# A longer planned distance between attention scores and the transposes of their softmax, and a third buffer for rows of p, in a one-core hybrid encoder layer

## The chip, the cores and the metric

The kernel runs on one core of a Trainium2 chip. The metric is the device time of one execution in microseconds (us). Five engines work side by side: TensorE (PE, with its weight loads shown as PEld), VectorE (DVE), ScalarE (ACT), GpSimd (POOL) and SyncE (SP), which issues DMAs. Each engine has a queue of its own, worked off in order; semaphores tie the queues together.

## The reference

One layer of a streaming encoder, for a prompt of 512 rows and a sample batch of 32 rows, which share all weights (544 columns in the kernel's transposed layout). All data are float32; D_MODEL is 1024, there are 16 heads of 64 in each mixer, the ConvFFN is 2816 wide.

```
h = rmsnorm(x)
z = h @ w_in                      # q_a k_a v_a q_b k_b v_b gate_a gate_b
# mixer A: 16 q heads on 4 kv heads, own chunk of 64 + 2 chunks before, ALiBi, a sink in the softmax
# mixer B: 16 heads, own chunk + 8 chunks before, learned relative bias
q, k = rmsnorm per head of q, k
p = softmax(q @ k.T * 64**-0.5 + bias)
o = p @ v
x = x + (sigmoid(gate_a) * o_a + sigmoid(gate_b) * o_b) @ w_out
[a | b] = causal depthwise conv3(rmsnorm(x) @ w_up)
x = x + (gelu(a) * b) @ w_down
```

The sample rows attend to given caches of k and v too. New rows of k, v and of the convolution are outputs as well.

## The kernel before

**Dense products.** The projection by `w_in` is cut into 52 tiles of 128 output rows, `w_out` into 8, `w_up` into 44, and so on. `dense` (L232) computes one tile in two halves of 272 columns, each in one PSUM bank. Float32 accuracy comes from a split of both operands into a high and a low part in the type fp32r: `triple` (L220) issues hi x hi, hi x lo and lo x hi, so that a half is 8 x 3 = 24 products and a tile 48. The moving operands are called xh and xl (s in `w_out` and behind), the weights w_hi and w_lo. `prep` (L192) makes them from a loaded w_raw: POOL rounds w_hi (L201), VectorE subtracts w_lo (L204); each has two buffers, so that a weight can be made only once the last product with the weight two tiles earlier is done. All matmuls are recorded in one helper line, L85, all transposes in L89.

**What is between the dense products.** A tile of q or k goes through `head_norm` (L401): ScalarE reads the bank twice (a square, L411, and z, L412), POOL splits the square (t_sqh L413, t_sql L414), PE takes two products with a block matrix of ones into a bank st, `newton` (L312) makes the reciprocal root of it (t_y and t_b; VectorE's part, L319, reads the bank again), POOL multiplies z by t_y (L421), VectorE writes zn (L422), and `write` splits it into the stacks q (L445, L446) or k (L429 to L431), of which one half is copied to the other partitions by a DMA (`dup`, L434).

An attention head of the prompt is `attend_prompt` (L528): four score tiles into four banks, from which VectorE writes p with the bias added and the row maximum taken (L501); the softmax in place on p (exponentials on ScalarE L485, the scaling by the reciprocal sum on POOL L493); transposes of p on PE into two or three banks, each evacuated as pt_h and pt_l (L511, L512); the output products with v into one more bank, and `fold` (L515; t_o L519, s L520). There are 16 such heads in mixer A and 16 in mixer B. `attend_sample` (L560) does the same for the sample rows of several heads at once, with p_s in place of p.

**What sets the order.** The class `Stream` (L69) keeps a clock of its own, in microseconds, that each recorded matmul moves on. An attention head is a generator; where it says `yield LAT_SOFT`, it is put aside until the clock has gone on by that amount. After each triple of a dense tile, `pe.step()` takes up one task that is due, or starts the next head of a queue. So the LAT constants say how many dense products are written between two steps of a head. The softmax itself is issued at a low priority (`LATER`). Behind that, the framework's scheduler takes the recorded program, its priorities, buffers and its own estimate of times, and decides the final order on every engine; the recorded order is thus its input and not its result.

**Banks and buffers.** Dense halves use a pool of 3 PSUM banks (`psd`); everything else, the norms, scores, transposes and outputs, shares 5 (`psa`). Tiles of the attention come from the pool `ap`, with two buffers each unless a number is given. `p` is a tile of 128 x 1280 float32 values, 5 KB in each partition.

**The end of the stretch.** The last products of `w_in` and the last heads end near 485 us. Then the `w_out` tiles begin: the first two are interleaved over three banks (L871 to L883) with the products of the gates (`s`, L827) cut into high and low parts as they come ready, and the results are added to x by VectorE (L898).

Of the kernel before, what the change touches and what calls it, by code (L numbers as in the profile page):

```python
# [8 lines left out]
F32 = mybir.dt.float32  # L9
# [44 lines left out]

LAT_FIRST, LAT_ROW = 9.15, 0.35
LAT_SQ, LAT_NORM, LAT_DMA = 2.9, 6.89, 3.63
LAT_Z, LAT_SOFT, LAT_PT = 6.55, 9.34, 4.75
LAT_SOFT_S, LAT_PTS = 8.46, 1.1
PACE_A, PACE_B, PACE_S = 7.09, 5.87, 1.44

WARM = 7
# [82 lines left out]
def body(ctx, tc, a, o):  # L144
# [16 lines left out]
    def bank(pool):  # L161
        return pool.tile([128, 512], F32, name="ps")
# [204 lines left out]
    ap = att.enter_context(tc.tile_pool(name="ap", bufs=2))  # L367
# [110 lines left out]
    def softmax(p, tiles, mx, sinkcol):  # L478

        n = len(tiles)  # L480
        nm = ap.tile([128, 4], F32, name="nm", bufs=3)[:, :n]
        V.tensor_scalar(nm, mx, -1.0, 1.0, ALU.mult, ALU.mult)  # L482
        sm = ap.tile([128, 4], F32, name="sm", bufs=4)[:, :n]
        for t, sl in enumerate(tiles):
            act(p[:, sl], p[:, sl], AF.Exp, bias=nm[:, t:t + 1], accum_out=sm[:, t:t + 1])  # L485
        if sinkcol is not None:
            es = ap.tile([128, 4], F32, name="es", bufs=3)[:, :n]
            act(es, nm, AF.Exp, bias=sinkcol)
            V.tensor_tensor(sm, sm, es, ALU.add)
        rc = ap.tile([128, 4], F32, name="rc", bufs=3)[:, :n]  # L490
        V.reciprocal(rc, sm)  # L491
        for t, sl in enumerate(tiles):
            G.tensor_scalar(p[:, sl], p[:, sl], rc[:, t:t + 1], 1.0, ALU.mult, ALU.mult)  # L493

    def scores(out, lhs, rhs, bias, floor, mx):
        ps = bank(psa)
        n = len(lhs)
        for i in range(n):
            mm(ps[:, :rhs[i].shape[1]], lhsT=lhs[i], rhs=rhs[i], start=i == 0, stop=i == n - 1)
        ps = ps[:, :out.shape[1]]  # L500
        V.tensor_tensor_reduce(out=out, in0=ps, in1=bias, op0=ALU.add, op1=ALU.max, scale=1.0,  # L501
                               scalar=floor, accum_out=mx)

    def transposed(p, blocks, n):

        ps = bank(psa)
        for src, dst in blocks:
            transpose(ps[:, dst:dst + 128], p[:, src:src + 128], ident)
        h = ap.tile([128, 512], F32R, name="pt_h", bufs=3)
        l = ap.tile([128, 512], F32R, name="pt_l", bufs=3)  # L510
        nc.scalar.copy(h[:, :n], ps[:, :n])  # L511
        V.tensor_tensor(l[:, :n], ps[:, :n], rr(h)[:, :n], ALU.subtract)  # L512
        return h, l

    def fold(po, dst, hh, n):  # L515

        own, other = ((slice(0, 64), slice(64, 128)), (slice(64, 128), slice(0, 64)))[hh]
        t = ap.tile([128, 512], F32, name="t_o", bufs=2)
        nc.scalar.copy(t[own, :n], po[other])  # L519
        V.tensor_tensor(dst[own], po[own], t[own, :n], ALU.add)  # L520
# [7 lines left out]
    def attend_prompt(q, kh, kl, bias, floor, sinkcol, geo, groups, vt, hh, dst, dh, scored, done):  # L528


        p = ap.tile([128, 1280], F32, name="p")
        mx = ap.tile([128, 4], F32, name="mx", bufs=4)
        tiles = []
        for t, (pc, k0, n, bc) in enumerate(geo):
            qs = q[:, 128 * t:128 * t + 128]
            scores(p[:, pc:pc + n], [qs, qs], [x[:, k0:k0 + max(n, 256)] for x in (kh, kl)], bias[:, bc:bc + n],
                   floor, mx[:, t:t + 1])
            tiles.append(slice(pc, pc + n))
        scored()
        with tc.high_priority(LATER):  # L540
            softmax(p, tiles, mx, sinkcol)
        yield LAT_SOFT
        pts = []
        for blocks, n, _ in groups:
            pts.append(transposed(p, blocks, n))
        yield LAT_PT
        po = bank(psa)
        started = False
        last = groups[-1][2][-1]
        for (h, l), (_, _, prods) in zip(pts, groups):  # L550
            for pr in prods:
                j, c, oc, w = pr
                for x in (h, l):
                    mm(po[:, oc:oc + w], lhsT=vt[:, j, hh, :, :], rhs=x[:, c:c + w],
                       start=not started, stop=pr is last and x is l, skip_group_check=True)
                    started = True
        fold(po, dst[:, :NP], dh, NP)
        done()
# [132 lines left out]
    def group_a(j, ka, va):  # L691
# [25 lines left out]
        for u in range(2):  # L717
            pe.reserve("q", 2, 5)
            st2 = [ap.tile([128, NP], F32R, name="q", bufs=5) for _ in range(2)]
            ready = []  # L720
            qready.append(ready)

            def sample(zn, u=u):
                for hh, own, other in pair_rows():
                    h = 2 * u + hh
                    nc.scalar.copy(qsam[own, h], zn[own])
                    V.tensor_tensor(qsam[other, h], zn[own], rr(qsam)[own, h], ALU.subtract)
            for hh in range(2):
                h = 4 * j + 2 * u + hh

                def start(bias, u=u, hh=hh, st2=st2, h=h):
                    sc = col("sink", h)
                    return attend_prompt(st2[hh], kh, kl, bias, sc, sc, a_geo, a_groups, vt, half,
                                         oa[u], hh, scored, finished)
                pe.queue(lambda h=h: fetch("bias", h, 512, a["alibi"][h]), start, (ready, ka[2], va[2]), PACE_A)
            dense(head_norm(0, load_q(st2, sample, ready)))
# [28 lines left out]
    def pair_b(i, ob, one):  # L765
# [48 lines left out]
        for hh in range(2):  # L814
            def start(bias, hh=hh):
                return attend_prompt(st2[hh], kh[hh], kl[hh], bias, -3.0e38, None, b_geo, b_groups, vt, hh,
                                     ob, hh, scored, finished)
            pe.queue(lambda hh=hh: fetch("bias", i, 512, a["rel"][2 * i + hh]), start, (qr, kr, vr), PACE_B)
# [413 lines left out]
```

## Time and profile before

| what | us |
|---|---|
| median of 3 runs (lowest, highest) | 924.7 (921.4, 926.1) |
| profiled execution, its time | 924.88 |
| profiled execution, its span in the trace | 923.0 |
| PE busy (multiplications) | 898.6 |
| PEld busy | 884.4 |
| DVE busy | 723.6 |
| ACT busy | 542.2 |
| POOL busy | 379.1 |

The mean granted clock of TensorE over the span was 0.994 of full speed. A busy engine is one that executes an instruction; the span is the time between the first and the last record of the execution. In the rows further down, a number in square brackets at a row's end is the time that the engine stood idle just before the instruction, followed by the instruction that released it.

### The profile page before, as it was taken

What the parts mean: (1) busy time and instruction counts of PE and PEld (TensorE: products, weight loads), DVE (VectorE), ACT (ScalarE), POOL (GpSimd) and SP (SyncE); (2) the same over time, 40 slices, a digit from 0 to 9 for tenths busy, and PEclk for the clock granted to TensorE, in tenths of its full rate; (3) what the DMA queues carried; (4) which work ended last, traced back from release to release, by engine and by line L of the source; (5) the groups of instructions that cost most, each with busy time, mean ns of one, the idle gap of its engine ahead of it and who ended that gap; (6) DMA issues with size and microseconds to landing.
All of it is one profiled execution on the core that took longest, in us unless ns stands there. A gap on an engine that the chain in (4) does not pass through costs nothing.

```text
span 923.0 us, 18908 instructions
## 1 busy us (share of the span) xinstructions
PE 898.6 (97%) x7085; PEld 884.4 (96%) x7085; DVE 723.6 (78%) x1471; ACT 542.2 (59%) x1285; POOL 379.1 (41%) x578
## 2 busy tenths in 40 slices
PE   8879999999999999999999999999999999999998
PEld 7879899989989999999999999999999999999998
DVE  7799876868888888998866558768777776886996
ACT  5568777778878777777764244344444443534542
POOL 6534457465876777766541103221222221100100
PEclk9999999999999999999999999999999999999999
DMA  6222222322334443434415222222222222332342
GB/s 216 83 82 88 71 90 85 101 81 75 109 118 122 135 124 109 129 110 136 133 59 168 89 92 92 92 77 85 92 93 92 84 87 83 96 101 81 119 145 67
DMA packets 40012, 94.38 MB, mean 102 GB/s; under 512 B 4944, under 2 KB 16240, under 8 KB 39920
## 3 DMA queue, kind: packets, MB, share of 16 engines
q1 hardware_dynamic: 39920, 93.17, 31.8%
q8 instruction: 56, 0.92, 0.4%
q14 instruction: 36, 0.29, 0.1%
HBM read 80.48 MB, written 7.10 MB: 95 GB/s over the span
## 4 chain that ended last, share of the span: by engine, by line
PE 76%; DVE 9%; ACT 4%; POOL 3%; issue 2%; DMA 0%; DVEq 0%; POOLq 0%
PE ps L85 73%; PE ps L89 3%; ACT p L485 2%; DVE q L446 1%; DVE zn L422 1%; DVE p L501 1%; DVE w_lo L204 1%; POOL p L493 1%; DVE s L254 1%; DVE t_b L319 1%; DVE k L431 1%; POOL t_sql L414 1%; POOL z L421 1%; DVE pt_l L512 0%; DMA k<-k 0%
## 5 line engine op out<-in xcount | busy, mean ns | idle before, releaser
L85 PE MATMUL ps<-xh,w_lo 128*128 128x272 f32 x1536 | 446.3, 292 | 5.1 <-DVE w_lo L204 5.1
L85 PE MATMUL ps<-xh,w_hi 128*128 128x272 f32 x1536 | 446.0, 292 | 2.7 <-ACT z L412 1.7
L85 PE MATMUL ps<-xl,w_hi 128*128 128x272 f32 x1536 | 446.3, 291 | 0.8 <-DVE xl L327 0.8
L85 PEld LDWEIGHTS ps<-xh,w_lo 128*128 128x128 f32 x1536 | 291.6, 190 | 6.5 <-DVE w_lo L204 6.0
L85 PEld LDWEIGHTS ps<-xh,w_hi 128*128 128x128 f32 x1536 | 291.5, 190 | 4.8 <-ACT z L412 1.9
L85 PEld LDWEIGHTS ps<-xl,w_hi 128*128 128x128 f32 x1536 | 292.0, 190 | 2.1 <-DVE xl L327 1.7
L204 DVE TENSOR_TENSOR w_lo<-w_raw,w_hi 128x1024 fp32r<-128x1024 f32 (+2 forms) x112 | 143.2, 1279 | 30.8 <-ACT w_hi L203 18.3
L201 POOL TENSOR_SCALAR w_hi<-w_raw 128x1024 fp32r<-128x1024 f32 (+2 forms) x62 | 66.6, 1075 | 90.2 <-PE ps L85 70.3
L493 POOL TENSOR_SCALAR p<-p,rc 128x256 f32<-128x256 f32 (+3 forms) x128 | 74.2, 596 | 41.4 <-DVE rc L491 38.0
L203 ACT CAST w_hi<-w_raw 128x1024 fp32r<-128x1024 f32 x50 | 52.6, 1051 | 64.9 <-issue 36.1
L85 PE MATMUL ps<-s,w_hi 128*128 128x272 f32 x448 | 84.0, 288 | 0.0
L485 ACT ACTIVATE p<-p,nm 128x256 f32<-128x256 f32 (+3 forms) x128 | 65.4, 514 | 27.8 <-DVE nm L482 27.7
L938 POOL TENSOR_SCALAR state_u<-u 128x2 f32<-128x2 f32 x44 | 17.1, 388 | 148.7 <-DVE u L935 148.7
L85 PE MATMUL ps<-s 128*128 128x272 f32 (+1 forms) x483 | 71.3, 293 | 1.7 <-DVE s L372 1.7
L85 PEld LDWEIGHTS ps<-s,w_hi 128*128 128x128 f32 x448 | 70.1, 188 | 0.0
L935 DVE TENSOR_TENSOR u<-ps,rstd 128x272 f32<-128x272 f32 x88 | 38.5, 441 | 39.6 <-PE ps L85 37.0
L85 PEld LDWEIGHTS ps<-s 128*128 128x128 f32 x483 | 65.1, 190 | 2.2 <-DVE s L372 1.7
L85 PE MATMUL ps<-s,w_lo 128*128 128x272 f32 x224 | 63.8, 288 | 0.0
L85 PE MATMUL ps<-k,q 128*128 128x256 f32 (+2 forms) x256 | 52.1, 308 | 3.5 <-DMA k<-k 1.8
L414 POOL TENSOR_TENSOR t_sql<-t_sq,t_sqh 128x272 fp32r<-128x272 f32 x52 | 52.7, 1014 | 3.7
L421 POOL TENSOR_TENSOR z<-z,t_y 128x272 f32<-128x272 f32 x52 | 42.7, 822 | 23.9 <-ACT t_y L316 21.7
L512 DVE TENSOR_TENSOR pt_l<-ps,pt_h 128x512 fp32r<-128x512 f32 (+1 forms) x80 | 45.6, 602 | 5.5 <-ACT pt_h L511 4.4
(166 smaller groups left out, 1635.1 us busy)
## 6 DMA issues: line engine op xcount, KB each, us to landing
w_raw<-in_w_in SPq DMA_DIRECT2D x50, 512.0 KB, 3.4
w_raw<-in_w_up SPq DMA_DIRECT2D x44, 512.0 KB, 3.3
w_raw<-in_w_pair SPq DMA_DIRECT2D x16, 512.0 KB, 3.4
k<-k SPq DMA_DIRECT2D x40, 128.0 KB, 2.3
bias<-in_rel SPq DMA_DIRECT2D x16, 256.0 KB, 2.7
w_raw<-in_w_out SPq DMA_DIRECT2D x8, 512.0 KB, 3.5
s<-in_x SPq DMA_DIRECT2D x15, 272.0 KB, 5.7
w_raw<-in_w_down SPq DMA_DIRECT2D x6, 512.0 KB, 3.3
```

The costliest lines, as they stand in the source:

```text
L85: return self.nc.tensor.matmul(out, lhsT=lhsT, rhs=rhs, **kw)
L89: return self.nc.tensor.transpose(out, src, ident)
L201: G.tensor_scalar(hi[:, c], raw[:, c], 1.0, 1.0, ALU.mult, ALU.mult)
L203: nc.scalar.copy(hi[:, c], raw[:, c])
L204: V.tensor_tensor(lo[:, c], raw[:, c], rr(hi)[:, c], ALU.subtract)
L414: G.tensor_tensor(sql, sq, rr(sqh), ALU.subtract)
L421: G.tensor_tensor(z, z, y, ALU.mult)
L485: act(p[:, sl], p[:, sl], AF.Exp, bias=nm[:, t:t + 1], accum_out=sm[:, t:t + 1])
L493: G.tensor_scalar(p[:, sl], p[:, sl], rc[:, t:t + 1], 1.0, ALU.mult, ALU.mult)
L512: V.tensor_tensor(l[:, :n], ps[:, :n], rr(h)[:, :n], ALU.subtract)
L935: V.tensor_tensor(u[:, 2 + c0:2 + c0 + cn], ps, rstd2[:, c0:c0 + cn], ALU.mult)
L938: G.tensor_scalar(state_u[:, m, 0:2], u[:, NP:NP + 2], 1.0, 1.0, ALU.mult, ALU.mult)
```

## The change

Three numbers are changed. `LAT_SOFT`, the planned time from the last score of a prompt head to the first transpose of its softmax, goes from 9.34 to 11.5; `LAT_SOFT_S`, the same for a sample batch, from 8.46 to 10.5; and the tile `p` of a prompt head gets three buffers instead of two. The computation is the same, and so is the number of matmuls.

```
-LAT_Z, LAT_SOFT, LAT_PT = 6.55, 9.34, 4.75
-LAT_SOFT_S, LAT_PTS = 8.46, 1.1
+LAT_Z, LAT_SOFT, LAT_PT = 6.55, 11.5, 4.75
+LAT_SOFT_S, LAT_PTS = 10.5, 1.1
...
-        p = ap.tile([128, 1280], F32, name="p")
+        p = ap.tile([128, 1280], F32, name="p", bufs=3)
```

The final order of the instructions is the same on PE for the first part of the program, up to some 98 us of the trace; from there to the first `w_out` tiles it is another one, on all engines. Three places of it follow.

VectorE, at the norm of a q tile and the first sample batch of mixer A (102 to 110 us of the trace before). Before:

```order
L422 SCALAR_TENSOR_TENSOR zn<-t_b,z 128x272
L446 TENSOR_TENSOR q<-zn,q 64x272
L204 TENSOR_TENSOR w_lo<-w_raw,w_hi 128x1024
L446 TENSOR_TENSOR q<-zn,q 64x272
L319 SCALAR_TENSOR_TENSOR t_b<-ps,eps,t_b 128x272
L520 TENSOR_TENSOR s<-ps,t_o 64x512
```

And with the change, on the same engine from the same zn on:

```order
L422 SCALAR_TENSOR_TENSOR zn<-t_b,z 128x272
L319 SCALAR_TENSOR_TENSOR t_b<-ps,eps,t_b 128x272
L446 TENSOR_TENSOR q<-zn,q 64x272 x2
L204 TENSOR_TENSOR w_lo<-w_raw,w_hi 128x1024
L520 TENSOR_TENSOR s<-ps,t_o 64x512
```

The operation t_b, which reads a norm's bank, moved from behind two splits of q and one of a weight to the place directly behind zn.

PE at the same place: the dense row that ends at 107 us (xh and xl are the split input rows, numbered by buffer), behind it before the two transposes of the sample's p_s:

```order
L85 MATMUL ps<-xh_160,w_lo 128x272
L85 MATMUL ps<-xh_165,w_hi 128x272
L85 MATMUL ps<-xl_166,w_hi 128x272
L85 MATMUL ps<-xh_165,w_lo 128x272
L89 MATMUL ps<-ident,p_s 80x128 x2
L85 MATMUL ps<-xh_109,w_hi 128x272
```

And with the change (the buffers of the rows are numbered lower by 5):

```order
L85 MATMUL ps<-xl_156,w_hi 128x272
L85 MATMUL ps<-xh_155,w_lo 128x272
L85 MATMUL ps<-k,q 128x256 x2
L85 MATMUL ps<-xh_160,w_hi 128x272
L85 MATMUL ps<-xl_161,w_hi 128x272
L85 MATMUL ps<-xh_160,w_lo 128x272
```

A score of a prompt head stands there now, six products ahead of the row's end, and takes the bank of the norm; the sample's transposes follow some 30 products later.

PE at the step from the last `w_in` products to `w_out` (495 to 499 us of the trace before). The rows on ps_7512 belong to the dense tile before; those on ps_7656 and ps_7682 are the first `w_out` tile, with w_hi_7498 and w_lo_7499. Before:

```order
L85 MATMUL ps_7512<-s_7487,w_lo_7377 128x272
L85 MATMUL ps_7512<-s_7493,w_hi_7376 128x272
L85 MATMUL ps_7512<-s_7494,w_hi_7376 128x272
L85 MATMUL ps_7512<-s_7493,w_lo_7377 128x272
L85 MATMUL ps_7656<-s_4603,w_hi_7498 128x272
L85 MATMUL ps_7656<-s_4604,w_hi_7498 128x272
L85 MATMUL ps_7682<-s_4603,w_hi_7498 128x272
L85 MATMUL ps_7682<-s_4604,w_hi_7498 128x272
L85 MATMUL ps_7656<-s_4603,w_lo_7499 128x272
```

And with the change, where the same weights are called w_hi_7480 and w_lo_7481, and those of the tile behind them w_hi_7486:

```order
L85 MATMUL ps_7494<-s_7475,w_lo_7377 128x272
L85 MATMUL ps_7494<-s_7533,w_hi_7376 128x272
L85 MATMUL ps_7494<-s_7534,w_hi_7376 128x272
L85 MATMUL ps_7494<-s_7533,w_lo_7377 128x272
L85 MATMUL ps_7656<-s_4583,w_hi_7480 128x272
L85 MATMUL ps_7656<-s_4584,w_hi_7480 128x272
L85 MATMUL ps_7682<-s_4583,w_hi_7480 128x272
L85 MATMUL ps_7682<-s_4584,w_hi_7480 128x272
L85 MATMUL ps_7721<-s_4583,w_hi_7486 128x272
L85 MATMUL ps_7721<-s_4584,w_hi_7486 128x272
L85 MATMUL ps_7656<-s_4583,w_lo_7481 128x272
```

Two products with the second weight moved ahead of the first one's w_lo. The last product with w_hi_7271, whose buffer the first weight here takes, stands 18 products ahead of this weight's first one before, and 7 with the change. On VectorE three of the four additions of L898 stand ahead of this w_lo before, and all four with the change.

## Rows read from the trace of the kernel before

**Rows 1.** The page, part 1: busy us, share of the span and number of instructions of each engine.

```profile
PE 898.6 (97%) x7085; PEld 884.4 (96%) x7085; DVE 723.6 (78%) x1471; ACT 542.2 (59%) x1285; POOL 379.1 (41%) x578
```

**Rows 2.** Busy time by stretch. The columns are the window (us from the start), its length, the busy us (and instructions) of PE, PEld, DVE, ACT and POOL, the granted clock of TensorE, the share of the DMA engines and GB/s.

```profile
96.00:480.00 384.00, 374.19 (x3000) 365.24 (x3000) 313.67 (x717) 295.65 (x837) 249.14 (x323) 1.00 0.34 105
110.00:114.00 4.00, 4.00 (x22) 4.00 (x22) 3.70 (x10) 2.84 (x9) 0.79 (x1) 0.57 0.12 49
114.00:480.00 366.00, 358.05 (x2883) 349.50 (x2882) 298.45 (x689) 282.42 (x798) 240.93 (x309) 1.00 0.35 107
480.00:486.00 6.00, 6.00 (x48) 5.92 (x47) 2.54 (x5) 2.33 (x6) 0.00 (x0) 1.00 0.29 91
```

**Rows 3.** The waits of PE from 96 to 500 us: who waits, for whom, us in all, how many, the longest.

```profile
PE ps L89 <- DVE t_b L319: 1.9, 1, 1.9
PE ps L85 <- DMA k<-k: 1.8, 1, 1.8
PE ps L85 <- ACT z L412: 1.7, 2, 1.4
PE ps L89 <- POOL p L493: 1.0, 2, 0.7
PE ps L85 <- POOL t_sql L414: 0.9, 2, 0.5
PE ps L85 <- DVE s L520: 0.8, 1, 0.8
PE ps L85 <- POOL t_sqh L413: 0.8, 1, 0.8
PE ps L85 <- DVE pt_l L512: 0.6, 2, 0.3
PE ps L89 <- DVE pt_l L512: 0.4, 1, 0.4
```

**Rows 4.** The waits of VectorE from 48 to 480 us, the line that writes p.

```profile
DVE p L501 <- PE ps L85: 11.3, 14, 2.2
```

**Rows 5.** The timeline of PE: the two transposes that waited for p.

```profile
180.99 0.33 PE L89 MATMUL ps<-ident,p 128*128 128x128 f32 x1 [0.30 <-POOL p L493]
...
336.14 0.33 PE L89 MATMUL ps<-ident,p 128*128 128x128 f32 x1 [0.69 <-POOL p L493]
```

**Rows 6.** The timeline around 107 us, of PE, VectorE and POOL, and behind it the group of line 422 (durations in ns: least, median, longest).

```profile
106.75 0.29 PE L85 MATMUL ps<-xh,w_lo 128*128 128x272 f32 x1
108.89 0.39 PE L89 MATMUL ps<-ident,p_s 128*80 128x128 f32 x2 [1.86 <-DVE t_b L319]
...
102.06 3.51 DVE L422 SCALAR_TENSOR_TENSOR zn<-t_b,z 128x272 f32<-128x272 f32 x1 [0.24 <-POOL z L421]
106.52 1.23 DVE L204 TENSOR_TENSOR w_lo<-w_raw,w_hi 128x1024 fp32r<-128x1024 f32 x1
108.24 0.50 DVE L319 SCALAR_TENSOR_TENSOR t_b<-ps,eps,t_b 128x272 f32<-128x272 f32 x1
...
102.38 1.04 POOL L201 TENSOR_SCALAR w_hi<-w_raw 128x1024 fp32r<-128x1024 f32 x1
104.50 0.76 POOL L414 TENSOR_TENSOR t_sql<-t_sq,t_sqh 128x272 fp32r<-128x272 f32 x1
...
L422 DVE SCALAR_TENSOR_TENSOR zn<-t_b,z x52: 406/466/3508, 41.2 to 453.2; 128x272 f32<-128x272 f32 x52
```

**Rows 7.** The timeline at the first scores of mixer B: the copies of k in SP's queue, the score that waited, and the stretch behind it as in rows 2.

```profile
258.14 3.50 SPq L434 DMA_DIRECT2D k<-k  x4
261.63 0.48 PE L85 MATMUL ps<-k,q 128*128 128x256 f32 x2 [1.85 <-DMA k<-k]
...
260.00:270.00 10.00, 8.37 (x62) 8.23 (x63) 7.10 (x18) 5.77 (x19) 9.13 (x10) 1.00 0.51 148
```

**Rows 8.** The timeline of PE: the two dense products that waited for a bank read into z.

```profile
310.98 0.39 PE L85 MATMUL ps<-xh,w_hi 128*128 128x272 f32 x1 [1.39 <-ACT z L412]
...
368.84 0.39 PE L85 MATMUL ps<-xh,w_hi 128*128 128x272 f32 x1 [0.26 <-ACT z L412]
```

**Rows 9.** The timeline at the step into `w_out`, of PE, POOL and VectorE.

```profile
495.65 0.29 PE L85 MATMUL ps<-s,w_hi 128*128 128x272 f32 x1
498.04 0.67 PE L85 MATMUL ps<-s,w_hi 128*128 128x272 f32 x4
498.54 0.29 PE L85 MATMUL ps<-s,w_lo 128*128 128x272 f32 x1
...
496.03 1.05 POOL L201 TENSOR_SCALAR w_hi<-w_raw 128x1024 fp32r<-128x1024 f32 x1 [8.80 <-PE ps L85]
498.15 1.09 POOL L201 TENSOR_SCALAR w_hi<-w_raw 128x1024 fp32r<-128x1024 f32 x1 [1.08 <-PE ps L85]
...
497.11 1.23 DVE L204 TENSOR_TENSOR w_lo<-w_raw,w_hi 128x1024 fp32r<-128x1024 f32 x1
```

**Rows 10.** The timeline of the last head's end: the copy of its output, the products with the gates and the casts behind them.

```profile
485.76 0.58 ACT L519 COPY t_o<-ps 64x512 f32<-64x512 f32 x1 [3.45 <-PE ps L85]
488.85 1.37 DVE L827 TENSOR_TENSOR s<-s 128x544 f32<-128x544 f32 x2 [0.36 <-ACT s L616]
490.89 1.28 ACT L430 CAST s<-s 128x544 fp32r<-128x544 f32 x2
```

## The prediction, made before the changed kernel had been run

> **What bounds the kernel now.** Read the page's shares first: TensorE (PE) is busy for 898.6 of 923.0 us, 97% [rows 1]. The multiplications themselves are the same before and after, so only the 24.4 us in which PE stands still, and stretches at the lower clock, are to be won or lost. The table by stages comes next: from 96 to 480 us, the stretch in which the change moves anything, PE is busy for 374.19 of 384.00 us, so 9.81 us is the most that fewer waits can give there [rows 2]. Ahead of 96 us the PE order of both kernels is the same, and behind 500 us too. The third view, PE's waits inside that stretch, says what these 9.81 us are, and here the change's own target is small: transposes that wait for the softmax rows p (POOL, L493) are 1.0 us in 2 waits [rows 3]. The rest is a bank held by t_b (1.9), a copy of k (1.8), the reading of banks into z (1.7), and small ones. In the waits of VectorE the line that writes p (L501) waits for PE's scores alone, never for a transpose to give a buffer of p back [rows 4]. So the third buffer removes no wait that exists.
>
> **What the change is worth by what it says.** In the two waits for p, PE stood 0.30 and 0.69 us [rows 5]. The planner's clock puts 2.16 us more between scores and transposes, but a scheduler decides behind it: counted in the two orders, the dense products between a head's last score and its first transpose are 61.8 on the mean before and 67.6 after (6 more; a product takes 6.00 / 48 = 0.125 us [rows 2], so 0.7 us); 19 heads gain, 4 stay, 9 lose. I take the two waits as gone: **-1.0** (bounds 0, as the heads that lose could wait in their place, and -1.0).
>
> **What the change is worth by what it moves.** Since the order of all engines behind 96 us is drawn anew, the larger waits have to be looked at one by one.
>
> *The wait at 107 us.* PE ends its row at 107.03 and starts the sample's two transposes at 108.89, held for 1.86 us by t_b (L319), which has to read the bank that they write. On VectorE t_b stood last behind zn (102.06, 3.51 us instead of its usual half), q, w_lo and q, and began at 108.24 [rows 6]. In the new order t_b stands directly behind zn, and on ScalarE the square that it reads ahead of the q casts instead of behind them. Even if zn is as slow again, t_b runs from 105.57 and ends near 106.1. PE's first user of that bank is now a score, 6 products earlier, at 107.03 - 6 x 0.125 = 106.3. So the wait goes: **-1.86** (bounds 0 and -1.86). The 3.51 us of zn lie over four POOL operations without a gap, 102.38 to 105.26 [rows 6]. The Trainium skill, SBUF — State Buffer, "Who interferes with whom", says that a VectorE operation with two inputs in SBUF and a GpSimd operation that reads SBUF lock each other out for a whole instruction; the trace agrees in kind, though zn was held over four of them and not one. By that rule with one instruction held, zn would end by some 103.9 and the wait would go as well.
>
> *The clock behind it.* From 110 to 114 us the granted clock is 0.57, in which 22 instructions ran, right behind that wait; with the clock at 1.00 the same work takes 4.00 x 0.57, so it cost **-1.7** [rows 2]. It goes with the wait (bounds 0 and -1.7). What makes it fall is not told by length alone: after the wait of 1.85 us at 261 the clock stayed at 1.00 [rows 7].
>
> *The copy of k.* The first scores of mixer B stood 1.85 us until 261.63 for the copies of k, issued from 258.14 over 3.50 us [rows 7]. Their place moves: counted in PE's own work from the second norm product of that k, they stood 9.4 us behind it before and 11.1 after. If the copies take as long, **-1.7** (bounds 0 and -1.85). The other pairs of mixer B then stand 10.9 us or more behind theirs, where the slowest chain needed 9.4 + 1.85 = 11.25, so some 0.3 us may come back; I leave it to the last term.
>
> *The banks read into z (L411, L412).* A dense product's next user of its bank came 1.17 and 1.63 us of PE work behind it in the two places that waited 1.39 and 0.26 us [rows 8]; so ScalarE needed 2.56 and 1.89 us. In the new order three places are this tight, 1.87, 1.91 and 1.97. At 1.89 to 2.56 us of need, each waits 0 to 0.7, 0.3 on the mean: 0.9 in place of 1.65, **-0.75** (bounds -1.65 and +0.4).
>
> *The step into w_out.* This one goes up. Before, the last product with the first w_out weights (w_hi_7271) stood 18 products ahead of their successor; POOL refilled the buffer from 496.03 to 497.08, and PE came for it at 498.04. Its w_lo ended at 498.34, for 498.54 [rows 9]. After, the last reader stands 7 products ahead and the next buffer's last reader one product ahead. On the old time base that product starts at 497.03; the old one, at 495.65, let POOL begin 0.38 later, so POOL begins at 497.41 and ends at 498.46 (0.5 us of wait with the signal); the second refill, which used to begin at 498.15, runs to 499.5 and PE, back since 498.55, wants it four products on, 499.05: 0.55. The w_lo now stands behind all four L898 adds, another 0.13. Together **+1.2** (bounds 0, and 2.9 if the clock falls after it).
>
> *A crowd at the 23rd head.* In the new order an output product follows its transposes by 1.7 us of PE work, where the least was 3.1 before, and three banks change hands within 2.4 us of that. By hand, the ScalarE queue there lets one of them wait: **+0.5** (bounds 0 and 2).
>
> *The rest.* The waits on t_sqh, t_sql, pt_l and s, 0.8 + 0.9 + 0.6 + 0.4 + 0.8 = 3.5 us [rows 3], are drawn anew with no sign that I can read; I keep the sum and add **+1.0** for places that I have not found (bounds -3.5 and +4).
>
> Hidden, and taken at nothing: the last head's output moves 24 products later, past the first w_out product; its chain (copy at 485.76, gate products, split until 492.17) took 6.4 us, of which three were the sigmoids that came between, and 57 products (7.1 us) lie between it and its first user now [rows 10]. If that cover were gone, PE would stand for the difference.
>
> **Sum.** -1.0 - 1.86 - 1.7 - 1.7 - 0.75 + 1.2 + 0.5 + 1.0 = -4.3. The profiled execution took 924.88 us, 1.9 of them around the span and 0.2 above the median of 924.7; that gives 920.6. Since most bounds lie on the side of less gain, I put it at **921.0**, 0.4% less. About 0.5% (4.6 us) is what a measurement of this kernel tells from no change, so the forecast lies on the border of it.
>
> **The rivals.** *The change doesn't do what it says* (chance 0.17): 0.7 us more per head and 9 heads with less, so the waits are only dealt out anew, with the same 9.8 us: 923 to 926.5. For it: only 1.0 us of PE's waits were for p. Against: the two largest have a named cause that the order takes away.
> *The clean case* (0.14): the new places at w_out and the 23rd head don't wait, and half of the rest goes: -7 to -9, so 916 to 918. Against it: the refill arithmetic, which has little play.
> *Slower: a bank wait per head* (0.08). Heads now live longer in the same five PSUM banks; the order has 27 places in the stretch where a bank changes hands within 3 us of PE work, 23 before. At such places PE waited 1.7 us in all before. If each of the 32 heads waited x for a bank, the price is 32x; it eats the 3.7 us at x = 0.12 us and is slower by over 0.5% from x = 0.26 us, some 930. Against it: the median gap is unchanged, 5.8 us.
> *Slower: the clock falls more often* (0.06). Each fall costs some 1.7 us [rows 2], and several short waits follow each other at w_out and the 23rd head; with four falls, 921.0 + 1.7 + 4 x 1.7 = 929.5, and it decides from there. For it: one fall stood behind a wait of 1.86 us; against: none stood behind 1.85, or anywhere else behind 114 us, where the clock is 1.00 throughout [rows 2, 7]. The Trainium skill, TensorE: Matmul & The Clock Gate, "A second HAM failure mode: psum-queue depth-cycling", tells of short idles between groups that make the clock swing; no stretch of this trace behind 114 us shows that.
>
> **Chances and range.** My forecast holds 0.55, from 917.5 to 924.5; 0.25 of it lies below 920.1 and 0.30 above. Faster by over 0.5%: 0.25 + 0.14, less 0.01 for a clean case that falls short, 0.38. Slower: 0.08 + 0.06 = 0.14. Within: 0.30 + 0.17 + 0.01 = 0.48. The range 916.5 to 927.5 leaves out the slower cases and a little of the clean one; the forecast's own is narrower, as given.
>
> **What would show it.** Right: no wait of the sample's transposes on t_b, clock 1.00 from 110 to 114, the wait on k below 0.4 us, none of transposes on p, three small ones on z below 0.7, and new waits for w_hi (POOL) and w_lo at 497 to 500, of 1.2 in all. Wrong: a wait of over 1.5 us at a place not named here, a second fall of the clock, or scores or output products that wait for banks head after head.

## The result, and the profile after

The changed kernel takes 927.77 us (median of 17 runs, 926.43 to 930.32), the kernel before 923.13 us (median of 17 runs, 920.79 to 926.1): a ratio of 1.0051, with a 95% interval of 1.0041 to 1.0061. It is slower by 4.6 us, where 0.4% less was forecast. The profiled execution of the changed kernel took 927.3 us with a span of 925.5 us, near its median; that of before, 924.88 us, turned out to lie 1.75 us above the median of its own 17 runs.

The page of the changed kernel, busy time by engine, answers to [rows 1]; the two rows of the table by stretch answer to [rows 2] (window, length, busy us and instructions of PE, PEld, DVE, ACT and POOL, granted clock, DMA share, GB/s):

```profile
PE 897.4 (97%) x7085; PEld 881.4 (95%) x7085; DVE 720.7 (78%) x1471; ACT 542.3 (59%) x1285; POOL 381.2 (41%) x578
...
96.00:480.00 384.00, 372.77 (x2987) 362.53 (x2986) 308.48 (x713) 294.37 (x832) 251.23 (x323) 1.00 0.34 104
110.00:114.00 4.00, 4.00 (x36) 4.00 (x35) 3.82 (x9) 2.77 (x5) 0.61 (x1) 1.00 0.01 4
```

PE stands still longer in the stretch that the change redraws: 384.00 - 372.77 = 11.23 us, where it was 9.81. From 110 to 114 us it ran 36 products where it ran 22, at the full clock.

PE's waits from 90 to 520 us of the changed kernel answer to [rows 3] (engine, tile and line waited for; us in all, times, longest):

```profile
PE ps L85 <- DVE mx L501: 2.9, 2, 1.6
PE ps L85 <- DVE pt_l L512: 2.4, 4, 1.4
...
PE ps L89 <- ACT s L292: 0.7, 1, 0.7
...
PE ps L89 <- DVE t_b L319: 0.5, 1, 0.5
...
PE ps L85 <- ACT s L292: 0.4, 1, 0.4
PE ps L89 <- DVE pt_l L512: 0.2, 1, 0.2
```

Three rows of before are not there any more: p (L493), z (L412), and t_b's 1.9. In their place stand two that were small or absent: mx (L501) is the reading of a bank of scores by VectorE, for which a later head's scores wait, and pt_l (L512) the reading of a bank of transposes. The row of pt_l on L85 is output products that wait for pt_l itself, their operand; the one on L89 is a transpose that waits for the bank. The longest of them on PE's timeline, with the idle time in brackets, and behind them the step into `w_out` that answers to [rows 9]:

```profile
117.98 0.46 PE L85 MATMUL ps<-pts,v_s 80*64 80x64 f32 x8 [1.33 <-ACT pts L574]
125.03 0.29 PE L85 MATMUL ps<-xl,w_hi 128*128 128x272 f32 x1
126.95 0.48 PE L85 MATMUL ps<-k,q 128*128 128x256 f32 x2 [1.64 <-DVE mx L501]
178.38 0.50 PE L85 MATMUL ps<-k,q 128*128 128x256 f32 x2 [1.31 <-DVE mx L501]
250.44 0.39 PE L85 MATMUL ps<-pt_l,v 128*128 128x256 f32 x1 [1.39 <-DVE pt_l L512]
310.36 0.50 PE L85 MATMUL ps<-pt_h,v 128*128 128x512 f32 x1 [0.38 <-ACT pt_h L511]
311.64 0.50 PE L85 MATMUL ps<-pt_l,v 128*128 128x512 f32 x1 [0.65 <-DVE pt_l L512]
376.85 0.50 PE L85 MATMUL ps<-k,q 128*128 128x256 f32 x2 [0.37 <-DMA k<-k]
...
499.19 0.77 PE L85 MATMUL ps<-s,w_hi 128*128 128x272 f32 x4 [0.31 <-POOL w_hi L201]
500.19 0.52 PE L85 MATMUL ps<-s,w_hi 128*128 128x272 f32 x2 [0.24 <-POOL w_hi L201]
501.26 0.39 PE L85 MATMUL ps<-s,w_lo 128*128 128x272 f32 x1 [0.56 <-DVE w_lo L204]
```

What VectorE, ScalarE and POOL did ahead of four of these waits, in the changed kernel:

```profile
112.44 1.28 ACT L616 ACT_TABLE_LOAD   x1
113.74 1.40 ACT L616 ACTIVATE s<-s,cols 128x544 f32<-128x544 f32 x2
115.15 1.28 ACT L620 ACT_TABLE_LOAD   x1
117.56 0.37 ACT L574 COPY pts<-ps 80x256 f32<-80x256 f32 x1
...
123.01 3.00 POOL L699 TENSOR_TENSOR s<-s 128x544 f32<-128x544 f32 x2
123.79 2.49 DVE L446 TENSOR_TENSOR q<-zn,q 64x240 fp32r<-64x240 f32 x2 [0.46 <-ACT q L445]
126.31 0.48 DVE L501 CUSTOM_DVE_ANT_0 p<-ps,bias,cols 128x256 f32<-128x256 f32 x1
...
176.69 1.23 DVE L204 TENSOR_TENSOR w_lo<-w_raw,w_hi 128x1024 fp32r<-128x1024 f32 x1
177.84 0.48 DVE L501 CUSTOM_DVE_ANT_0 p<-ps,bias,cols 128x256 f32<-128x256 f32 x1
...
248.47 1.20 DVE L204 TENSOR_TENSOR w_lo<-w_raw,w_hi 128x1024 fp32r<-128x1024 f32 x1
```

At 118 us the sample's pts stood behind the sigmoids of a gate and the two table loads around them. At 127 us the reading of the scores (L501, from 126.31) stood behind two splits of q, which took 2.49 us beside two products on POOL. At 178 us it stood behind a w_lo, and at 250 us the reading into pt_l (L512, from 249.70) behind another. The causes differ; common is that a short reading of an attention bank stood behind something longer in its engine's queue.

### The profile page after: what moved, and what is told of

Same layout as the page of the kernel before. It is cut to its first block, busy times and chain, and to the rows that moved or that the text cites. A ratio compares the mean times of both kernels' runs of the same rounds, so it can differ in the third digit from the quotient of the medians.

```text
span 925.5 us, 18915 instructions
## 1 busy us (share of the span) xinstructions
PE 897.4 (97%) x7085; PEld 881.4 (95%) x7085; DVE 720.7 (78%) x1471; ACT 542.3 (59%) x1285; POOL 381.2 (41%) x578
## 4 chain that ended last, share of the span: by engine, by line
PE 53%; DVE 3%; ACT 2%; POOL 1%; DMA 1%; issue 1%; DVEq 0%
PE ps L85 53%; ACT p L485 1%; POOL p L493 1%; PE ps L89 1%; DMA k<-k 1%; DVE p L501 0%; DVE w_lo L204 0%; DVE zn L422 0%; DVE k L431 0%; DVE pt_l L512 0%; DMA bias<-in_rel 0%; DVE q L446 0%; POOL s L827 0%; DVE nm L482 0%; POOL z L421 0%
## 5 line engine op out<-in xcount | busy, mean ns | idle before, releaser
L85 PE MATMUL ps<-xh,w_lo 128*128 128x272 f32 x1536 | 444.1, 290 | 6.3 <-DVE w_lo L204 6.3
L85 PE MATMUL ps<-xh,w_hi 128*128 128x272 f32 x1536 | 443.8, 291 | 1.5 <-ACT xh L326 0.7
L85 PE MATMUL ps<-xl,w_hi 128*128 128x272 f32 x1536 | 444.5, 290 | 0.8 <-DVE xl L327 0.8
L85 PEld LDWEIGHTS ps<-xh,w_lo 128*128 128x128 f32 x1536 | 290.1, 189 | 7.8 <-DVE w_lo L204 7.2
L85 PEld LDWEIGHTS ps<-xh,w_hi 128*128 128x128 f32 x1536 | 290.2, 190 | 3.1 <-ACT xh L326 1.0
L85 PEld LDWEIGHTS ps<-xl,w_hi 128*128 128x128 f32 x1536 | 290.5, 189 | 2.2 <-DVE xl L327 1.7
L493 POOL TENSOR_SCALAR p<-p,rc 128x256 f32<-128x256 f32 (+3 forms) x128 | 76.5, 614 | 41.9 <-DVE rc L491 26.2
L85 PE MATMUL ps<-s,w_hi 128*128 128x272 f32 x448 | 84.4, 289 | 0.6 <-POOL w_hi L201 0.6
L85 PE MATMUL ps<-s 128*128 128x272 f32 (+1 forms) x483 | 71.3, 293 | 1.7 <-DVE s L372 1.7
L85 PEld LDWEIGHTS ps<-s,w_hi 128*128 128x128 f32 x448 | 70.0, 188 | 1.0 <-POOL w_hi L201 1.0
L85 PEld LDWEIGHTS ps<-s 128*128 128x128 f32 x483 | 65.1, 190 | 2.2 <-DVE s L372 1.7
L85 PE MATMUL ps<-s,w_lo 128*128 128x272 f32 x224 | 63.4, 289 | 0.6 <-DVE w_lo L204 0.6
L85 PE MATMUL ps<-k,q 128*128 128x256 f32 (+2 forms) x256 | 53.8, 310 | 4.7 <-DVE mx L501 2.9
L512 DVE TENSOR_TENSOR pt_l<-ps,pt_h 128x512 fp32r<-128x512 f32 (+1 forms) x80 | 46.1, 600 | 8.0 <-ACT pt_h L511 7.7
L414 POOL TENSOR_TENSOR t_sql<-t_sq,t_sqh 128x272 fp32r<-128x272 f32 x52 | 50.2, 964 | 3.7
```

The costliest lines, as they stand in the source:

```text
L85: return self.nc.tensor.matmul(out, lhsT=lhsT, rhs=rhs, **kw)
L414: G.tensor_tensor(sql, sq, rr(sqh), ALU.subtract)
```

## The experiments

What the runs have to tell apart: whether the change is slower because of the longer distance, because of the third buffer, or because any redrawn order gets waits of its own. Each time is the median of the run's executions, and each ratio is against the kernel before, run in the same series.

### Each part alone, and two controls

The first two take one part each. The other two move LAT_SOFT by 0.25 us up and down, two products, which gives or takes no room to speak of, but draws the order anew.

```
e1_lat_only    LAT_SOFT 11.5, LAT_SOFT_S 10.5, p with 2 buffers
e2_p3_only     LAT_SOFT 9.34, LAT_SOFT_S 8.46, p with bufs=3
e3_nudge_up    -LAT_Z, LAT_SOFT, LAT_PT = 6.55, 9.34, 4.75
               +LAT_Z, LAT_SOFT, LAT_PT = 6.55, 9.6, 4.75
e4_nudge_down  +LAT_Z, LAT_SOFT, LAT_PT = 6.55, 9.1, 4.75
```

> LAT_SOFT 11.5 and LAT_SOFT_S 10.5 as in the changed kernel, p with two buffers as before. Theory A (every redrawn order deals out some 10 to 14 us of waits behind 96 us at other places, and the order before is a good draw): slower by 0.2 to 0.6%, 925 to 929 us, with waits at places that are not those of the changed kernel. Theory B (heads that live longer wait for banks and for late evacuations because of the longer distance): the same as the changed kernel, 927 to 929 us. Theory C (the third buffer of p does the harm): as before, within 0.2%, 922 to 925 us.

Measured: 937.69 us, ratio 1.0151 (1.0132 to 1.0170). Slower than the changed kernel by 10 us.

> p with three buffers, the LAT numbers as before. Theory A: the order is drawn anew from the middle of mixer A on, so slower by 0.1 to 0.5%, 924 to 928 us, or by luck no change. Theory B: as before, within 0.2%. Theory C: as the changed kernel, 927 to 929 us.

Measured: 932.13 us, ratio 1.0086 (1.0069 to 1.0102).

> LAT_SOFT 9.6 in place of 9.34 (two products more in the plan), all else as before: a control that redraws the order without giving or taking room. Theory A: it moves by an amount of the size of the change's own, 0.1 to 0.5%, mostly slower (924 to 928 us), through waits at new places. Theories B and C: within 0.1% of before.

Measured: 925.84 us, ratio 1.0020 (1.0003 to 1.0036).

> LAT_SOFT 9.1 in place of 9.34 (two products fewer in the plan), all else as before: the control to the other side. Theory A: slower by 0.1 to 0.5% (924 to 928 us), through waits at new places that have little to do with p. Theories B and C: within 0.1% of before, or slower by the waits for p alone, 1 us at most.

Measured: 933.26 us, ratio 1.0098 (1.0082 to 1.0114).

Two products more or fewer in the plan cost 2.1 and 9.5 us; each part of the change alone costs more than both together. So theory C falls, since the third buffer slows one pair of orders (923.73 to 932.13) and speeds the other (937.69 to 927.77), and theory A is so far the better one. It was too mild in size: it allowed 0.6% and saw 1.5%. The third buffer is not without effect, as the prediction had it, because it takes part in the drawing of the order, though no wait for a buffer of p was there to remove. (With two buffers at the longer distance, VectorE's writing of p waits once, 0.5 us, for a transpose to give a buffer back; that is little beside 10 us.)

### Other distances, and the clock

```
e5_after_nudge  the changed kernel with LAT_SOFT 11.6
e6_mid          LAT_SOFT 10.4, LAT_SOFT_S 9.5, p with bufs=3
e7_long         LAT_SOFT 13.5, LAT_SOFT_S 12.5, p with bufs=3
```

> The changed kernel with LAT_SOFT 11.6 in place of 11.5, one product more in the plan. Theory A (each order is a draw; what counts is where the evacuations of banks fall, not the distance): it moves against the changed kernel by 0.2 to 1%, either way, somewhere from 922 to 937 us, with waits at other places. Theory B (the distance itself costs): within 0.15% of the changed kernel, 926.5 to 929 us.

Measured: 937.15 us, ratio 1.0136 (1.0114 to 1.0159), 9.4 us more than the changed kernel for one product in the plan.

> LAT_SOFT 10.4 and LAT_SOFT_S 9.5, half of the change, p with three buffers. Theory A: anywhere from 922 to 937 us, in no order with the runs at 9.34 and 11.5. Theory B: between before and the changed kernel, 924.5 to 927 us.

Measured: 934.30 us, ratio 1.0117 (1.0098 to 1.0137).

> LAT_SOFT 13.5 and LAT_SOFT_S 12.5, twice the change, p with three buffers. Theory A: 922 to 937 us, not plainly above the changed kernel. Theory B: slower than the changed kernel by as much again or more, 931 to 936 us, with more waits of scores and output products for banks than any other.

Measured: 935.42 us, ratio 1.0126 (1.0105 to 1.0147).

The times don't follow the distance (9.1: 933, 9.34: 923, 9.6: 926, 10.4: 934, 11.5: 928, 11.6: 937, 13.5: 935). But the waits for VectorE's readings, mx and pt_l, taken apart from the others, fall into two groups by distance (table below), and that is what theory A alone doesn't say. Of all of them the changed kernel is the fastest with a distance of 10.4 or more.

> The kernel before once more, for the clock. If the fall of the granted clock at 110 to 114 us comes with the wait of 1.86 us at 107 us each time, as the prediction took it, this execution shows the same wait and the same stretch at 0.57. If the fall is a matter of the single execution, the wait is there again and the clock stays at 1.00 behind it.

Measured: 921.06 us, with a span of 919.2. Its rows at 107 us, of VectorE, PE and the stretch behind; then the same place in the run with the third buffer alone, and in the one with LAT_SOFT 9.6, whose orders on PE are still that of before there (they part from it near 130 and 181 us):

```profile
100.97 1.66 DVE L422 SCALAR_TENSOR_TENSOR zn<-t_b,z 128x272 f32<-128x272 f32 x1 [0.27 <-POOL z L421]
107.07 0.39 PE L89 MATMUL ps<-ident,p_s 128*80 128x128 f32 x2 [1.09 <-DVE t_b L319]
107.00:117.00 10.00, 9.93 (x85) 9.75 (x86) 8.71 (x28) 8.68 (x20) 5.14 (x5) 1.00 0.16 54
```

```profile
109.96 0.39 PE L89 MATMUL ps<-ident,p_s 128*80 128x128 f32 x2 [1.85 <-DVE t_b L319]
110.00:120.00 10.00, 10.00 (x84) 9.57 (x85) 8.84 (x28) 9.41 (x23) 5.38 (x5) 1.00 0.15 51
```

```profile
110.89 0.39 PE L89 MATMUL ps<-ident,p_s 128*80 128x128 f32 x2 [1.86 <-DVE t_b L319]
111.00:121.00 10.00, 10.00 (x84) 9.57 (x84) 8.84 (x28) 9.41 (x23) 5.38 (x5) 1.00 0.14 50
```

The same program shows a wait of 1.09 us here instead of 1.86, since zn took 1.66 us and not 3.51, and the clock stays at 1.00. The length of the wait doesn't decide it either: after waits of 1.85 and 1.86 us the clock stays at 1.00 in the two runs shown. Two more runs, with LAT_SOFT 9.1 and with the sample's distance alone (10.5, below), have the order of before up to this wait and another one behind it: both wait 1.86 us, and the granted clock is 0.57 from 109.5 to 113.5 us in the first and 1.00 from 108 to 118 us in the second. So of five waits of this size, that of before among them, two have a fall behind them, and the fall is a matter of the single execution. The next head starts from there 2.5 us earlier than in the other execution of before: 0.77 of the wait, and 1.7 of the clock.

### Which part of the distance, and what holds the banks

Theory B2, formed on the runs so far: a longer distance trades waits for p for waits for VectorE's readings, mx and pt_l.

```
e9_soft_only    LAT_SOFT 11.5, LAT_SOFT_S 8.46, p with bufs=3
e10_softs_only  LAT_SOFT 9.34, LAT_SOFT_S 10.5, p with bufs=3
e11_long12      LAT_SOFT 12.5, LAT_SOFT_S 10.5, p with bufs=3
e12_after_wlo_halves, in prep of the changed kernel:
-            V.tensor_tensor(lo[:, c], raw[:, c], rr(hi)[:, c], ALU.subtract)
+            for h in [c] if n < 2 or n >= 58 else [slice(0, 512), slice(512, 1024)]: V.tensor_tensor(lo[:, h], raw[:, h], rr(hi)[:, h], ALU.subtract)
```

> LAT_SOFT 11.5 alone, LAT_SOFT_S 8.46 as before, p with three buffers. Theory A (a draw alone): 922 to 938 us, and the waits of PE for VectorE's readings of attention banks (for mx, L501, and for pt_l, L512, together 0.3 to 2.4 us in the orders at 9.1 to 9.6 and 5.5 to 8.0 us at 10.4 to 13.5 so far) anywhere between 0 and 8 us. Theory B2 (a longer distance of the prompt heads trades waits for p for waits for those readings): these two together at 4.5 us or more, waits for p below 1.5 us. If the sample's distance is what does it, they are below 2.5 us.

Measured: 937.43 us, ratio 1.0143 (1.0123 to 1.0163). PE's waits of the two kinds in it:

```profile
PE ps L85 <- DVE pt_l L512: 4.1, 6, 1.7
PE ps L85 <- DVE mx L501: 2.0, 4, 0.7
PE ps L89 <- DVE pt_l L512: 1.6, 2, 1.3
```

That is 7.7 us, and no row for p.

> LAT_SOFT 9.34 as before, LAT_SOFT_S 10.5 alone, p with three buffers. Theory A: 922 to 938 us, mx and pt_l together anywhere between 0 and 8 us. Theory B2: mx and pt_l together at 2.5 us or less, as in all orders at 9.1 to 9.6, with waits for p of 0.5 to 4 us; the time still moves by the draw. If the sample's distance does it, 4.5 us or more.

Measured: 932.25 us, ratio 1.0090 (1.0069 to 1.0111). The same kinds, and p:

```profile
PE ps L89 <- POOL p L493: 3.4, 7, 0.7
PE ps L85 <- DVE mx L501: 1.6, 1, 1.6
PE ps L85 <- DVE pt_l L512: 1.0, 3, 0.5
PE ps L89 <- DVE mx L501: 0.5, 1, 0.5
```

3.1 us, a little over the bound of 2.5 that B2 set, and far from the 4.5 of the other theory. It is the distance of the prompt heads that goes with these waits.

> LAT_SOFT 12.5, LAT_SOFT_S 10.5, p with three buffers. Theory A: 922 to 938 us, mx and pt_l anywhere. Theory B2: mx and pt_l together at 4.5 us or more, hardly a wait for p, and a time above 927 us.

Measured: 934.50 us, ratio 1.0112 (1.0091 to 1.0133); mx and pt_l 5.8 us, p 1.5 us (more than B2 had expected).

> The changed kernel, with w_lo (L204, 1.2 us on VectorE, in front of which L501 and L512 stood at 178 and 250 us) made in two halves of 512 columns for the weights of w_in and w_out, so that a reading of a bank stands behind at most 0.65 us of it. It costs some 56 x 0.06 = 3.4 us of VectorE, which has room. If the blocks of 1.2 us are what holds the banks, mx and pt_l together fall from 5.5 us to below 3 us and the time to 922 to 926 us. If it is a matter of the draw, they stay anywhere between 3 and 8 us, and the time at 925 to 938 us.

Measured: 935.86 us, ratio 1.0128 (1.0109 to 1.0148); mx and pt_l 6.0 us. Halving the blocks of 1.2 us doesn't lower the waits; the guess, taken from the rows at 178 and 250 us, gets no support. The edit also draws the order anew, on PE from 30 us on, so it isn't one order with and without the blocks.

### Load, banks, phase, and one more order of the short kind

```
e13_less_vector_work, in prep of the changed kernel:
+            if n < 2 or n >= 58: V.tensor_tensor(lo[:, c], ...)
+            else: V.tensor_tensor(lo[:, :512], ...); nc.sync.dma_start(out=rr(lo)[:, 512:], in_=rr(hi)[:, 512:])
e14_six_banks       the changed kernel with psd bufs=2, psa bufs=6
e15_one_pace_more   LAT_SOFT 15.2, LAT_SOFT_S 8.46, p with bufs=4
e16_nudge_945       the kernel before with LAT_SOFT 9.45
```

> The changed kernel, where VectorE makes only columns 0 to 511 of w_lo for the weights of w_in and w_out; the other columns are a copy of w_hi by a DMA, so the low products of k chunks 4 to 7 are left wrong. PE's work is the same, VectorE has some 0.6 us less for each tile, about 30 us of 314 in the stretch. If VectorE's load makes its readings late: PE's waits for mx and pt_l together fall from 5.5 us to below 2.5 us. If the order (what stands ahead of a reading) or the number of banks does it: 4 us or more remain.

Measured: 920.86 us, ratio 0.9970 (0.9954 to 0.9986). A line was added to the file, so its L502 and L513 are L501 and L512:

```profile
PE ps L85 <- DVE pt_l L513: 1.5, 2, 1.2
PE ps L89 <- DVE pt_l L513: 0.9, 1, 0.9
PE ps L85 <- DVE mx L502: 0.8, 2, 0.4
```

3.2 us, between the two bounds; the time is 6.9 us below the changed kernel. VectorE is busy for 693.2 us of this execution, where the changed kernel has 720.7. The kernel leaves out half of each low part, and its order is another one on PE from 30 us on, so the run doesn't take load and order apart.

> The changed kernel with two banks for dense halves and six for attention in place of three and five. If the longer distance costs because five banks are too few for heads that overlap more, PE's waits for mx (scores that want a bank) fall to below 1 us, and those for z, s and w (dense halves) rise by more than that. If the data come late whatever the banks, mx and pt_l together stay at 4 us or more.

Measured: 946.16 us, ratio 1.0251 (1.0218 to 1.0285).

```profile
PE ps L85 <- ACT pt_h L511: 3.9, 4, 2.0
PE ps L85 <- DVE pt_l L512: 3.9, 3, 1.9
PE ps L85 <- ACT s L292: 3.4, 2, 2.0
PE ps L85 <- ACT z L412: 3.3, 2, 1.8
```

The waits for mx are gone, which fits scores that are short of a bank, though in a single order, which is another one from 8 us on. Those for pt_l and pt_h are not: these are output products that wait for their operand, and a bank more doesn't help them (with 0.7 us of transposes, mx and pt_l are 4.6 us together). The dense halves wait 6.7 us for s and z with two banks, so this is no way out.

> LAT_SOFT 15.2, which is 9.34 and one pace of mixer B (5.87), LAT_SOFT_S 8.46, p with four buffers. If the phase in which a head's transposes meet the scores of later heads is what counts, the waits for mx and pt_l together are 3 us or less, as at 9.34. If it is the length (more heads alive at once), 5.5 us or more, and the time 932 us or more. Waits for p: none.

Measured: 931.60 us, ratio 1.0091 (1.0062 to 1.0121); mx and pt_l 2.3 + 0.9 + 0.2 = 3.4 us, no wait for p. It lies between what phase and length had called for, nearer to phase: the longest distance of all has fewer of these waits than each one from 10.4 to 13.5.

> LAT_SOFT 9.45, all else as before. If short distances keep the waits for mx and pt_l low whatever the draw: together 3 us or less. Of the time the draw decides: 922 to 934 us.

Measured: 932.96 us, ratio 1.0107 (1.0078 to 1.0135); mx and pt_l 0.4 us, as expected, and waits for p, k and s in their place.

### A quarter of w_lo on POOL

```
-            V.tensor_tensor(lo[:, c], raw[:, c], rr(hi)[:, c], ALU.subtract)
+            for e, h in [(V, c)] if n < 2 or n >= 58 else [(V, slice(0, 768)), (G, slice(768, 1024))]: e.tensor_tensor(lo[:, h], raw[:, h], rr(hi)[:, h], ALU.subtract)
```

> The kernel before, with columns 768 to 1023 of w_lo made on POOL and the others on VectorE for the weights of w_in and w_out. VectorE has some 0.3 us less for each tile (14 us of 314 in the stretch), POOL some 0.8 us more (35 us on 249). If VectorE's load is what counts: 918 to 924 us. If POOL's two-input operations hold VectorE up by as much as they take from it, or if the draw decides: 924 to 936 us, with waits for t_sq and w in their place.

Measured: 935.59 us, ratio 1.0128 (1.0106 to 1.0149).

```profile
PE ps L85 <- DVE pt_l L512: 4.9, 4, 2.2
PE ps L85 <- DVE mx L501: 2.2, 4, 1.3
PE ps L89 <- DVE pt_l L512: 0.8, 1, 0.8
PE ps L89 <- DVE mx L501: 0.3, 1, 0.3
...
PE 903.0 (97%) x7085; PEld 886.5 (95%) x7085; DVE 715.2 (77%) x1471; ACT 543.3 (58%) x1285; POOL 430.9 (46%) x634
```

> The same edit on the changed kernel. If VectorE's load is what counts: the waits for mx and pt_l together fall from 5.5 us to below 4 us and the time to 921 to 926 us. If POOL holds VectorE up in turn, or the draw decides: 926 to 938 us.

Measured: 940.69 us, ratio 1.0183 (1.0157 to 1.0208); mx and pt_l 8.4 us.

VectorE got less relief than planned. Over the whole execution it is busy for 715.2 us in the first of the two runs, 8.4 less than before [rows 1]; in the second it is busy for 725.7, 5.0 more than in the changed kernel (720.7), so that run tests no relief at all. POOL is busy for 430.9 and 427.2 us, where it was 379.1 and 381.2. With a little less load, then, the waits for VectorE's readings went from 1.0 to 8.2 us at the short distance: they are not a matter of its load alone, nor do they need a long distance. Whether e13 gained by its 27.5 us less load or by its order stays open; the relief here is too small to tell, the work added to POOL is a rival of its own, and the order is another one on PE from 30 us on in both runs.

### The orders side by side

Worked out from the views of PE's waits: the sums of the rows for mx and pt_l (L501, L512) and for p and p_s (L493); all is the sum of the brackets of PE behind 93 us.

| order | median us | mx, pt_l | p | all |
|---|---|---|---|---|
| 9.1 (e4) | 933.26 | 2.5 | 3.5 | 13.1 |
| 9.34, before | 923.13 | 1.0 | 1.0 | 9.8 |
| 9.34, 3 buffers (e2) | 932.13 | 0.8 | 3.2 | 15.0 |
| 9.34, sample 10.5 (e10) | 932.25 | 3.1 | 3.4 | 13.2 |
| 9.45 (e16) | 932.96 | 0.4 | 2.6 | 14.1 |
| 9.6 (e3) | 925.84 | 0.3 | 0.5 | 12.0 |
| 10.4 (e6) | 934.30 | 8.0 | 0.4 | 15.6 |
| 11.5, the change | 927.77 | 5.5 | 0 | 12.3 |
| 11.5, 2 buffers (e1) | 937.69 | 7.1 | 2.9 | 19.0 |
| 11.5, sample 8.46 (e9) | 937.43 | 7.7 | 0 | 17.6 |
| 11.6 (e5) | 937.15 | 6.4 | 1.3 | 15.2 |
| 12.5 (e11) | 934.50 | 5.8 | 1.5 | 14.1 |
| 13.5 (e7) | 935.42 | 5.9 | 0 | 14.6 |
| 15.2, sample 8.46, 4 buffers (e15) | 931.60 | 3.4 | 0 | 14.3 |

The six orders up to 9.6 have 0.3 to 3.1 us of mx and pt_l, the seven from 10.4 to 13.5 have 5.5 to 8.0, with two buffers or three, and nothing lies between; the one at 15.2 has 3.4 and doesn't fit. The means of the six and the seven are 1.35 and 6.6 us, those of p 2.4 and 0.9, those of all waits 12.9 and 15.5, those of the times 929.9 and 934.9. So a longer distance, up to 13.5, goes with some 1.5 us less for p, as it says, and with some 5 us more for VectorE's readings. In the times this is less clear: there is a scatter of 10 us in each group, the two overlap from 927.8 to 933.3 us, and the kernels before and after are each the lowest of theirs. Nor do the brackets carry all of it: against before, the other orders up to 13.5 have 2.2 to 9.2 us more of them and take 2.7 to 14.6 us longer.

## Why the prediction was wrong, point by point

**The places it named, on the side of the gain.** It asked for no wait on p, and there is none (term -1.0, measured -1.0). The wait of 107 us is gone (-1.86). The copy of k waits 0.37 where it waited 1.85 (-1.7, measured -1.5). No dense product waits for a bank read into z; one waits 0.36 for a bank read into s in the same way (-0.75, measured -1.3). These steps held, the last by more than forecast.

**The places it named, on the side of the loss.** The step into `w_out` was put at +1.2, with POOL twice and w_lo once; the rows show 0.31 + 0.24 + 0.56 = 1.11, by those three. The 23rd head was put at +0.5; its output products at 365.58 us wait 0.16.

**The clock.** This is the first step that failed. The full clock from 110 to 114 us is there as forecast, but it is hardly a gain against the median: the fall belonged to the profiled execution. Five profiles have the order of before on PE through this place (the two of before, the third buffer alone, and LAT_SOFT 9.45 and 9.6), and one of them has the fall; the wait itself is 1.09 and 1.11 us in two of them and not 1.86. The sum was made from an execution that lay 1.75 us above its own median, and took as the kernel's what was that execution's. Of two waits of the same size the prediction had seen that one had a fall behind it and the other none; that should have halved the term. The same execution also hides a part of the miss: the sum of -4.3, taken from the median of 923.13, would have given 918.8, which is 8.9 us below the measured time, where 921.0 is 6.8 below it.

**The rest.** This is the step that decided. The prediction kept the small waits at 3.5 us and added 1.0 for places that it had not found. In the changed kernel everything that it did not name is 12.28 - 0.37 - 0.36 - 1.11 - 0.16 = 10.28 us, 6.8 us more in place of 1.0. Five places make 6.7 of the 10.28: 1.33, 1.64, 1.31, 1.39 and 0.38 + 0.65, in the rows above. The prediction had named a wait of over 1.5 us at a new place as a sign of being wrong; the 1.64 at 126.95 us is one. The order was read for the places that waited before; a place that had not waited before could be found only by going through the new order's queues of VectorE and ScalarE, and there that was done for one head alone. The brackets behind 93 us add up to 9.80 before and 12.28 after: 2.5 us more, where the sum without the clock's term had 2.6 less. That is 5.1 of the 8.9 us.

**What the brackets leave out.** Two products that are the same in both kernels, one ahead of the redrawn stretch and one behind it, in the kernel before and, under it, in the changed one:

```profile
69.08 0.44 PE L85 MATMUL ps<-xh,w_lo 128*128 128x272 f32 x1 [2.93 <-DVE w_lo L204]
510.08 0.42 PE L85 MATMUL ps<-s,w_hi 128*128 128x272 f32 x2
```

```profile
68.06 0.56 PE L85 MATMUL ps<-xh,w_lo 128*128 128x272 f32 x1 [2.97 <-DVE w_lo L204]
512.65 0.42 PE L85 MATMUL ps<-s,w_hi 128*128 128x272 f32 x2
```

That is 441.00 and 444.59 us: 3.6 us more, though one had the extra fall of the clock (1.7) and the brackets differ by 2.5 alone. So 3.6 + 1.7 - 2.5 = 2.8 us are lost where the rows show PE busy. Some 1 us of that is explained: the product at 125.03 us is drawn with 0.29 us, but without a wait the next would have started 0.125 later; it started 1.92 later, so 1.8 us were lost and the bracket says 1.64. With 20 brackets instead of 13, each 0.15 short, that makes 1.05. The other 1.7 us are not in pauses too short for a bracket. Worked out from the starts of all products between the two: take for each step from one product to the next the median step of its pair of kinds in both kernels (a score behind a dense product, and so on); without the brackets and the falls of the clock, the steps exceed these medians by 16.0 us in both kernels. What differs is the sum of the medians, by 1.6 us: other kinds of products stand next to each other, that is, the attention's products break up the dense rows in another way. The prediction took the brackets for the whole. Of the 8.9 us these 2.8 are the second part, and about 1 us is left for the clock's term.

**The rivals.** The mechanism of *a bank wait per head*, given 0.08, comes nearest to what the runs show, by half: 2.9 us are scores that wait for a bank, and 2.4 are output products that wait for their operand pt_l, not for a bank. Its form was wrong: it isn't a small wait at each of the 32 heads but a few of over 1 us, 4.5 us more in all. What the prediction held against it, the median gap between uses of a bank, did not change; the waits sit at a few tight places, of which a median says nothing. *The change doesn't do what it says* had the dealing-out right, and had the sum of it wrong, as if it were always 9.8 us: the orders of the table have 9.8 to 19.0 us. *The clock falls more often* didn't happen behind 96 us in the profiled execution. The range was too narrow for this reason above all: it allowed 4 us for unfound places, where 6.8 came, and orders whose plans differ by a product or two differ by 2 to 10 us.

**What stays open.** Why a longer distance goes with more of these waits. Shortage of banks may make the part of the scores (none with six banks, in one order). Halving w_lo's blocks didn't lower them. Load on VectorE alone doesn't make them, and how much of them it makes is not shown; the run at 15.2 speaks for the phase in which transposes meet later heads' scores, without settling it, since it is one order. Whether a kernel faster than both is to be had was tried in one way, the quarter on POOL, and that was slower.

## What to carry to other kernels

Where a planner's number feeds a scheduler, a change of it buys a new order, and the first thing to measure is what orders alone cost: two nudges that mean nothing, one to either side, moved this kernel by 2.1 and 9.5 us, where the change moved it by 4.6. A forecast from the places that waited before finds the gain and misses the loss; go through the new order for readings of shared banks that stand behind longer work, on every engine, or widen the range by the scatter of the orders. And before a fall of the clock is counted as a gain, look whether a second execution of the same kernel has it.

## What the runs showed of the hardware

The clock's lower level came and went at the same place, with one order of the products ahead of it: behind waits of 1.85 and 1.86 us the granted clock was 1.00 in three runs, and 0.57 over 4 us, most of it at the lower of its two levels (1.2 of 2.4 GHz), in two others. And the same zn on VectorE took 3.51 us in one execution and 1.66 us in another, with POOL busy beside it in both; at 123.79 us of the changed kernel two splits of q took 2.49 us beside two products on POOL of 3.00 us together, all with two operands in SBUF, and ended 0.27 us behind them (126.28 and 126.01). The Trainium skill, SBUF — State Buffer, "Who interferes with whom", tells of such a lock between VectorE and GpSimd for a whole instruction; the rows fit it, and show besides that the time for which VectorE is held is not the same in each execution.
